# The opening of a two-layer diffusion backbone: the modulation's loads in one run, small products between its matrix products, and another order behind them

## The chip, the cores and the metric

The kernel runs on one core of a Trainium2 chip. The metric is the device time of one execution in microseconds (us); the time given is the median of several runs. TensorE is called PE in the profile, VectorE DVE, ScalarE ACT, GpSimd POOL, and SyncE's queue, which issues all the loads and stores here, SPq.

## The reference

Two layers over 1024 latent tokens and 256 context tokens of width 1024, in float32. What concerns the change is the beginning of a layer:

```python
silu_c = jax.nn.silu(c)
mod = silu_c @ w_ada[l] + b_ada[l]                       # 6 x 1024 values
sh1, sc1, g1, sh2, sc2, g2 = jnp.split(mod[:, None, :], N_MOD, axis=-1)
h = rmsnorm(x, norm1_g[l]) * (1.0 + sc1) + sh1           # the same for the context with c_ctx
y, yc = token_mixers(h @ w_in[l], hc @ w_in[l], ...)     # gated linear memory and neighbourhood attention
x = x + g1 * (y @ w_out[l])
...                                                      # norm2, a squared-ReLU MLP, final norm
```

So no product with `w_in` can start before the sums of squares of x, and the first 2048 columns of `w_ada` (sh1 and sc1), have been worked off.

## The kernel before

Everything lies with features on the partitions: x is 8 feature tiles of 128, and its 1280 tokens are three groups: group 0 the 256 context tokens, groups 1 and 2 the 512 latent tokens each. A float32 product is taken as three (`mm3`, lines 94 to 96): each operand is split into a high part (a cast on ACT, line 1112 or 88) and the rest (a subtraction on DVE, line 1113 or 89), and high x high, high x low and low x high are added up in PSUM.

`opening` (layer 0 only) is ordered by hand: inside it each engine runs its instructions, and SyncE its transfers, in the order in which the code writes them. What comes behind it is ordered by a planner, which may put a later instruction into a place where an engine's queue would wait. `issue_after(i)` holds the instructions traced in its block behind `i`. The opening consists of

- `load_x`: the loads of x by group; `raws`: the first projection's weights `w_kvg` (keys, values and gates of the first head pair) in three pieces, 864, 864 and 576 columns;
- `ada`: two generators, `first` for column blocks 0 and 2 of `w_ada` and `second` for 1 and 3, that is shift and scale of feature tiles 0 to 3 (A) and 4 to 7 (B). Each loads eight tiles of 512 KB ("wada", six buffers for both generators together), multiplies each with silu(c) (line 158), and at its end copies the sums ("arow", line 185), transposes them (line 188) and adds the bias, which gives the columns of `mod` and the gain `A`. `steps(g, n)` takes n steps of a generator; steps 1 to 6 only load, steps 7 and 8 multiply and load, 9 to 14 multiply, 15 ends;
- `squares` (lines 1657 to 1659): the squares of a group on ACT, added in pairs on DVE and summed over partitions by products with ones; `rstd` (lines 297 and 298) takes 1/sqrt of it, `scale` (line 1664) multiplies x by it;
- `norm`: modulates feature tiles, even ones on ACT (line 1676), odd ones on DVE (line 1674), and splits each with `parts`; `self.normed` is the cast of the last one;
- `project`: part of the first projection, by token pair i (256 tokens: pair 0 is group 0, pairs 1 and 2 are group 1, 3 and 4 are group 2), feature tiles ks and half u; a feature tile costs one half three products of 288 columns.

Behind it `mixers` runs: it stores silu(c) to DRAM (`sscr`, two transfers of 1024 single values, line 1590), starts the loads of the further modulation (`fill`), projects token pair 4, turns keys and takes gates (`mlstm_kv`), and projects the values of the attention (`na_values`, weights `w_nv` in two pieces).

Of the kernel before, what the change touches and what calls it, by code (L numbers as in the profile page):

```python
# [11 lines left out]
F32 = mybir.dt.float32  # L12
# [14 lines left out]
KT = D // 128  # L27
# [20 lines left out]
class Kern:  # L48
# [1537 lines left out]
    def mixers(self, l, xsrc, hi, lo, need_ctx, W, accs, Wv):  # L1586
        self.wide = 0
        if l == 0:
            for v in range(2):
                self.nc.sync.dma_start(self.sscr[v, :].rearrange("(k p) -> p k", p=128), self.silu[:, :, v])  # L1590
            self.fill = self.ada(l, range(6, 10), "q")
            self.rows = self.ada_rows(l, range(4, 6), range(2))
        self.gt, self.mst, self.nst = None, {}, {}
        with self.open(name=f"mix{l}", side="right") as self.mx:
            with self.open(name=f"mkv{l}") as self.mp:
                self.cosT = self.load(self.mx, "cos", [128, 8, 32])
                self.sinT = self.load(self.mx, "sin", [128, 8, 32])
                self.sel = self.load(self.mx, "sel", [128, 16])
                kv = self.mlstm_kv(l, hi, lo, W, accs)
                with self.open(name=f"gt{l}", side="right") as tp_:  # L1600
                    gates = self.gates(l, tp_)
                    next(gates)

                    with self.tc.issue_after(self.normed.ins) if l == 0 else contextlib.nullcontext():
                        for i in range(NT // 2):
                            next(kv)
                            if i > 2:
                                next(gates)
                        next(kv)
                    values = self.na_values(l, hi, lo, Wv + self.value_weights(l, range(len(Wv), 2)))  # L1610
                    next(gates)
                    next(gates)
                    run_all(values)
                    with self.behind():
                        run_all(gates)
                W = self.joint_weights(l, 0)
                with self.behind():
                    first = self.project_j(W, 0, hi, lo, 512 if need_ctx else 256)
                with self.open(name=f"mout{l}") as self.mb:
                    self.setup_out(l)  # L1620
                    with self.behind():
                        run_all(kv)
                    Wq, keys = self.mlstm_out(l, hi, lo, need_ctx, W, first)
            with self.open(name=f"na{l}") as self.np_:
                yh, yl = self.alloc_act()
                W, xt = [], []
                self.na(l, hi, lo, need_ctx, Wq, keys, self.ahead(l, 0 if need_ctx else 1, xsrc, yh, yl, W, xt))
        return yh, yl, W, xt

    def opening(self, xp, ap0, xsrc, hi, lo):  # L1630


        nc, d = self.nc, self.d
        self.wide, self.ntmp = 0, 8
        x = self.alloc_x(xp, (0, 1, 2))
        self.setup()
        self.load_x(x, xsrc, (0, 1))
        chunks, raws = ((0, 864), (864, 864), (1728, 576)), []
        for o, n in chunks:
            raws.append(self.wp.tile([128, 1024], F32, name="wraw", bufs=WRAW) if o < 1728 else ap0.tile([128, n], F32, name="wraw2"))  # L1640
        for z in range(2):
            nc.sync.dma_start(raws[z][:, :864], d["w_kvg"][0][:, z * 864:z * 864 + 864])
        first, second = (self.ada(0, blocks, "mm", ap0, 6) for blocks in ((0, 2), (1, 3)))

        def steps(g, n):
            for _ in range(n):
                next(g)

        steps(first, 6)

        def squares(gi, q):
            p, n = self.bank("mm"), GROUPS[gi][1]
            q.extend((p, n))
            for f in range(0, KT, 2):
                sq = [self.sp.tile([128, 512], F32, name="tmp", bufs=self.ntmp) for _ in range(2)]
                for z, t in enumerate(sq):
                    nc.scalar.activation(t[:, :n], xf(x, gi, f + z), AF.Square)
                nc.vector.tensor_add(sq[0][:, :n], sq[0][:, :n], sq[1][:, :n])
                nc.tensor.matmul(p[:, :n], self.ones[:], sq[0][:, :n], start=f == 0, stop=f == KT - 2)
                yield  # L1660

        def scale(gi, r, fs=range(KT)):
            for f in fs:
                nc.vector.tensor_mul(xf(x, gi, f), xf(x, gi, f), r[:, :GROUPS[gi][1]])

        def norm(todo):

            sh = self.mod[:, 0:8, :]

            def modulation(gi, f):  # L1670
                xs, v = xf(x, gi, f), 1 if gi == 0 else 0
                a, b = self.A[0][:, f, v:v + 1], sh[:, f, v:v + 1]
                if f % 2:
                    nc.vector.tensor_scalar(xs, xs, a, b, ALU.mult, ALU.add)
                else:
                    nc.scalar.activation(xs, xs, AF.Identity, bias=b, scale=a)

            modulation(*todo[0])
            for n, (gi, f) in enumerate(todo):
                if n + 1 < len(todo):  # L1680
                    modulation(*todo[n + 1])
                self.normed = self.parts(xf(x, gi, f), hi[f][gi][:], lo[f][gi][:])

        q, A, B, accs = [[], [], []], range(4), range(4, 8), {}

        def project(i, ks, u):
            accs[i] = self.project_g(W, i, hi, lo, "q", accs.get(i), ks, (u,))

        run_all(squares(0, q[0]))
        more = squares(1, q[1])  # L1690
        steps(more, 2)
        r0 = self.rstd(*q[0])
        steps(more, 1)
        steps(first, 1)
        steps(more, 1)
        steps(first, 1)
        self.load_x(x, xsrc, (2,))
        nc.sync.dma_start(raws[2][:], d["w_kvg"][0][:, 1728:])
        r1 = self.rstd(*q[1])
        scale(0, r0)  # L1700
        for z in range(2):
            self.less_last(raws[z], chunks[z][1], 288)
        scale(1, r1, A)
        W = [self.split_raw(raws[z], chunks[z][1]) for z in range(2)]
        scale(1, r1, B)
        for z in range(6):
            steps(first, 1)
            steps(second, 1)
        self.less_last(raws[2], chunks[2][1], 288)
        steps(first, 1)  # L1710
        norm([(0, f) for f in A])
        for u in range(2):
            project(0, A, u)
        rest = squares(2, q[2])
        norm([(1, f) for f in A])
        for i in (1, 2):
            for u in range(2):
                steps(rest, 1)
                project(i, A, u)
                steps(second, 1)  # L1720
        r2 = self.rstd(*q[2])
        W.append(self.split_raw(raws[2], chunks[2][1]))
        steps(second, 4)
        scale(2, r2, range(3))
        steps(second, 1)
        norm([(0, f) for f in B])
        for u in range(2):
            project(0, B, u)
        norm([(1, f) for f in B])
        for i in (1, 2):  # L1730
            for u in range(2):
                project(i, B, u)
        scale(2, r2, range(3, KT))
        norm([(2, f) for f in range(KT)])
        accs[3] = [self.bank("mm") for _ in range(2)]
        for k in range(KT):
            for u in range(2):
                project(3, (k,), u)
        return W, accs, self.value_weights(0, range(1))

    def run(self):
        nc, d = self.nc, self.d
        PS = bass.MemoryType.PSUM
        with self.open(name="pad", side="right") as pad, self.open(name="const") as self.cp, self.open(name="w") as self.wp, \
# [12 lines left out]
            xsrc = d["xT"]  # L1757
            hi, lo = self.alloc_act()
            with self.open(name="x0") as xp, self.open(name="sp0") as self.sp, self.open(name="ada0") as ap0, self.tc.manual_schedule():
                W, accs, Wv = self.opening(xp, ap0, xsrc, hi, lo)  # L1760
            self.ntmp = 3
            for l in range(DEPTH):
                need_ctx = l < DEPTH - 1
                groups = (0, 1, 2) if need_ctx else (1, 2)
                yh, yl, W, xt = self.mixers(l, xsrc, hi, lo, need_ctx, W, accs, Wv if l == 0 else [])
                mod, A = self.mod, self.A
                hid, xmid = hids[l], xmids[l]
                ada = chain(*(self.ada_rows(*a) for a in ((l, range(10, 12), range(2)), (l + 1, range(4), range(2)), (l + 1, range(4, 12), range(1))) if need_ctx))
                hi, lo = self.alloc_act()
# [8 lines left out]
                start, finish = self.down(l, hid, we, alloc)  # L1778
# [110 lines left out]
def run_all(g):  # L1889
    for _ in g:  # L1890
        pass
# [19 lines left out]
WRAW = 2  # L1911
# [128 lines left out]
```

## Time and profile before

| | |
|---|---|
| median of 3 runs | 2864.13 us (2863.14 to 2865.72) |
| the profiled execution | 2859.85 us, of which the span of the profile 2857.9 us |
| instructions | 45593 |
| PE busy | 2807.8 us, 98% of the span |
| DVE, ACT, POOL busy | 2201.7 us, 1276.6 us, 111.9 us |
| DMA | 497.39 MB, mean 174 GB/s |
| granted PE clock, mean | 0.995 |

A row of the order of time has the start in us from the span's start, the duration in us (of a merged run of rows, all of it), the engine, the line, the operation, the tiles written and read, the shape, and how many were merged; the idle time ahead of it and what ended that stand in brackets. Neighbouring products overlap, so their distance is shorter than the duration of one. A row of windows has, for each stretch, the busy us and the number of instructions of each engine, then the granted clock of PE (1.00 is full), the DMA engines' mean busy share and GB/s. A row of waits has the waiting engine and line, what it waited for, the us in total, how many waits, and the longest.

### The profile page before, as it was taken

Reading aid. Unit: us, or ns where it says so; the run is one execution under the profiler, and the core shown is the slowest. Engines: PE = TensorE matmul, PEld = TensorE weight load, DVE = VectorE, ACT = ScalarE, POOL = GpSimd, SP = SyncE. Lnnn points to the kernel's source line nnn. Section 1 sums busy time; section 2 is a strip of 40 time slices with the busy share of each in tenths; the row PEclk is TensorE's granted clock in tenths of the full one; section 3 lists DMA queues with packets and bytes.
Section 4 is the critical chain, followed back from the end, with each engine's and each line's share of the span. In section 5 each row is a group of like instructions: output and inputs, shape, how many; then the busy total and the mean of one; then the engine's idle time right before and its main releaser. Section 6 shows DMA issues by size and latency. Waiting matters only on the chain. (4 is left out here: it accounts for less than half of the span.)

```text
span 2857.9 us, 45593 instructions
## 1 busy us (share of the span) xinstructions
PE 2807.8 (98%) x16560; PEld 2375.8 (83%) x16560; DVE 2201.7 (77%) x4909; ACT 1276.6 (45%) x2472; POOL 111.9 (4%) x191
## 2 busy tenths in 40 slices
PE   7999999999999999999999999999999999999998
PEld 4877778888888888888889988878988788888888
DVE  5779988776698777689878778878786887768774
ACT  4333335565453333434545333335564533344453
POOL 0100000011000000000000101000010000000000
PEclk8999999999999999999999999999999999999999
DMA  7333333336447555798977222223355454479672
GB/s 243 125 132 128 133 104 108 91 114 203 138 149 246 198 195 192 247 341 295 328 264 279 71 70 88 72 76 120 113 156 193 130 183 155 145 263 320 200 256 97
DMA packets 279263, 497.39 MB, mean 174 GB/s; under 512 B 23648, under 2 KB 119904, under 8 KB 279040
## 3 DMA queue, kind: packets, MB, share of 16 engines
q1 hardware_dynamic: 279040, 494.50, 51.8%
q8 instruction: 130, 2.13, 0.3%
q14 instruction: 93, 0.76, 0.1%
HBM read 398.82 MB, written 95.59 MB: 173 GB/s over the span
## 5 line engine op out<-in xcount | busy, mean ns | idle before, releaser
L94 PE MATMUL q<-ah,whi 128*128 128x512 f32 (+1 forms) x1472 | 549.4, 373 | 0.5 <-ACT whi L1112 0.5
L96 PE MATMUL q<-ah,wlo 128*128 128x512 f32 (+1 forms) x1472 | 547.0, 372 | 0.7 <-DVE wlo L1113 0.5
L95 PE MATMUL q<-al,whi 128*128 128x512 f32 (+1 forms) x1472 | 547.6, 372 | 0.0
L94 PE MATMUL mm<-ah,whi 128*128 128x512 f32 (+1 forms) x1120 | 387.0, 346 | 0.4 <-DVE nq L859 0.2
L95 PE MATMUL mm<-al,whi 128*128 128x512 f32 (+1 forms) x1120 | 384.8, 344 | 0.0
L96 PE MATMUL mm<-ah,wlo 128*128 128x512 f32 (+1 forms) x1120 | 384.6, 343 | 0.0
L96 PEld LDWEIGHTS q<-ah,wlo 128*128 128x128 f32 x1472 | 277.3, 188 | 49.9 <-DVE wlo L1113 1.3
L94 PEld LDWEIGHTS q<-ah,whi 128*128 128x128 f32 x1472 | 277.5, 188 | 49.7 <-issue 1.7
L95 PEld LDWEIGHTS q<-al,whi 128*128 128x128 f32 x1472 | 277.5, 189 | 48.4 <-issue 1.4
L94 PE MATMUL mm<-whi,ah 128*128 128x512 f32 (+2 forms) x832 | 308.0, 370 | 1.6 <-ACT va L810 1.6
L95 PE MATMUL mm<-wlo,ah 128*128 128x512 f32 (+2 forms) x832 | 297.9, 358 | 0.4 <-DVE wlo L89 0.3
L96 PE MATMUL mm<-whi,al 128*128 128x512 f32 (+2 forms) x832 | 297.9, 358 | 0.0
L94 PEld LDWEIGHTS mm<-ah,whi 128*128 128x128 f32 x1120 | 212.0, 189 | 28.0 <-issue 2.0
L96 PEld LDWEIGHTS mm<-ah,wlo 128*128 128x128 f32 x1120 | 212.0, 189 | 25.1 <-issue 0.2
L95 PEld LDWEIGHTS mm<-al,whi 128*128 128x128 f32 x1120 | 212.0, 189 | 24.6 <-issue 0.2
L1112 ACT CAST ah<-raw 128x512 fp32r<-128x512 f32 (+1 forms) x264 | 143.5, 566 | 126.0 <-PE q L96 51.8
L1113 DVE TENSOR_TENSOR al<-raw,ah 128x512 fp32r<-128x512 f32 (+1 forms) x264 | 157.8, 622 | 29.9 <-ACT ah L1112 29.2
L94 PEld LDWEIGHTS mm<-whi,ah 128*128 128x128 f32 x832 | 157.1, 189 | 27.1 <-ACT va L810 2.4
L96 PEld LDWEIGHTS mm<-whi,al 128*128 128x128 f32 x832 | 156.9, 189 | 23.8
L95 PEld LDWEIGHTS mm<-wlo,ah 128*128 128x128 f32 x832 | 157.3, 189 | 21.3 <-DVE wlo L89 1.8
L94 PE MATMUL q<-th,whi 128*128 128x512 f32 x384 | 150.4, 392 | 2.1 <-DVE s L1277 2.0
L95 PE MATMUL q<-x,whi 128*128 128x512 f32 x384 | 150.6, 392 | 1.1 <-DVE x L1113 1.1
(306 smaller groups left out, 5237.3 us busy)
## 6 DMA issues: line engine op xcount, KB each, us to landing
raw<-w SPq DMA_DIRECT2D x168, 512.0 KB
raw<-hid SPq DMA_DIRECT2D x104, 512.0 KB
wada<-w_adaT SPq DMA_DIRECT2D x96, 512.0 KB
wraw<-w SPq DMA_DIRECT2D x80, 512.0 KB
hid<-hb SPq DMA_DIRECT2D x128, 256.0 KB
hid<-ht SPq DMA_DIRECT2D x96, 256.0 KB
w<-gscr SPq DMA_DIRECT2D x36, 512.0 KB
wada<-w_ada SPq DMA_DIRECT2D x32, 512.0 KB
```

Of the source, the lines that this page charges most:

```text
L94: mm(out, lh, rh, start=start, stop=False, skip_group_check=True)
L95: mm(out, lh, rl, start=False, stop=False, skip_group_check=True)
L96: mm(out, ll, rh, start=False, stop=stop, skip_group_check=True)
L1112: ins = self.nc.scalar.copy(hi, src)
L1113: self.nc.vector.tensor_sub(lo, src, fview(hi))
```

## The change

In the opening, `second`'s tiles are loaded right behind `first`'s: the load of x's group 2 goes from ahead of them to behind them, and the load of the third piece of `w_kvg` to behind `second`'s fourth tile. `warm(n)` is new: n products of the matrix of ones with the silu tile (128 x 256), written to the bank that token pair 0 will use. One stands behind each of six pairs of steps, one ahead of `first`'s end, and two behind the next two steps of `second`; those are nine in the code. `second`'s products now run ahead of and between the first half's projections, which for pair 1 go feature tile by feature tile; group 2's squares, which ran between the first half's projections, come behind the second half of group 0; the second half of pairs 1 and 2 goes feature tile by feature tile too. The weights of the values are loaded in the opening, but split in `mixers`, behind the second step of the kv loop. The two stores of silu stand in a block `issue_after(self.normed.ins)`. All sums have the same terms in the same arithmetic.

```diff
     def mixers(self, l, xsrc, hi, lo, need_ctx, W, accs, Wv):
         if l == 0:
-            for v in range(2):
-                self.nc.sync.dma_start(self.sscr[v, :].rearrange("(k p) -> p k", p=128), self.silu[:, :, v])
+            with self.tc.issue_after(self.normed.ins):
+                for v in range(2):
+                    self.nc.sync.dma_start(self.sscr[v, :].rearrange("(k p) -> p k", p=128), self.silu[:, :, v])
...
                             if i > 2:
                                 next(gates)
+                            if Wv and i == 1:
+                                Wv = [self.split_raw(Wv[0], 1024)]
...
         q, A, B, accs = [[], [], []], range(4), range(4, 8), {}
+        accs[0] = [self.bank() for _ in range(2)]
 
         def project(i, ks, u):
-            accs[i] = self.project_g(W, i, hi, lo, "q", accs.get(i), ks, (u,))
+            accs[i] = self.project_g(W, i, hi, lo, "q" if i < 3 else "mm", accs.get(i), ks, (u,))
+
+        def warm(n):
+            for _ in range(n):
+                nc.tensor.matmul(accs[0][0][:, 0:256], self.ones[:], self.silu[:].rearrange("p k c -> p (k c)"), start=True, stop=True, skip_group_check=True)
...
-        self.load_x(x, xsrc, (2,))
-        nc.sync.dma_start(raws[2][:], d["w_kvg"][0][:, 1728:])
...
         for z in range(6):
             steps(first, 1)
             steps(second, 1)
-        self.less_last(raws[2], chunks[2][1], 288)
+            warm(1)
+            if z == 3:
+                nc.sync.dma_start(raws[2][:], d["w_kvg"][0][:, 1728:])
+        warm(1)
         steps(first, 1)
+        for z in range(2):
+            steps(second, 1)
+            warm(1)
+        self.load_x(x, xsrc, (2,))
         norm([(0, f) for f in A])
         for u in range(2):
             project(0, A, u)
-        rest = squares(2, q[2])
+        steps(second, 2)
         norm([(1, f) for f in A])
-        for i in (1, 2):
+        for f in A:
             for u in range(2):
-                steps(rest, 1)
-                project(i, A, u)
-                steps(second, 1)
-        r2 = self.rstd(*q[2])
+                project(1, (f,), u)
+            steps(second, 1)
+        self.less_last(raws[2], chunks[2][1], 288)
         W.append(self.split_raw(raws[2], chunks[2][1]))
-        steps(second, 4)
-        scale(2, r2, range(3))
+        project(2, A, 0)
         steps(second, 1)
+        project(2, A, 1)
         norm([(0, f) for f in B])
         for u in range(2):
             project(0, B, u)
-        norm([(1, f) for f in B])
-        for i in (1, 2):
-            for u in range(2):
-                project(i, B, u)
+        run_all(squares(2, q[2]))
+        norm([(1, 4), (1, 5)])
+        r2 = self.rstd(*q[2])
+        scale(2, r2, range(3))
+        norm([(1, 6), (1, 7)])
+        for f in B:
+            for i in (1, 2):
+                for u in range(2):
+                    project(i, (f,), u)
         scale(2, r2, range(3, KT))
         norm([(2, f) for f in range(KT)])
-        accs[3] = [self.bank("mm") for _ in range(2)]
-        for k in range(KT):
+        for f in range(KT):
             for u in range(2):
-                project(3, (k,), u)
-        return W, accs, self.value_weights(0, range(1))
+                project(3, (f,), u)
+        raw = self.wp.tile([128, 1024], F32, name="wraw", bufs=WRAW)
+        nc.sync.dma_start(raw[:], d["w_nv"][0, :, :1024])
+        return W, accs, raw
```

More of the change, by code (lines that the diff above doesn't have):

```diff
@@ L1759, in run @@
             with self.open(name="x0") as xp, self.open(name="sp0") as self.sp, self.open(name="ada0") as ap0, self.tc.manual_schedule():
-                W, accs, Wv = self.opening(xp, ap0, xsrc, hi, lo)
+                W, accs, raw = self.opening(xp, ap0, xsrc, hi, lo)
             self.ntmp = 3
@@ L1764, in run @@
                 groups = (0, 1, 2) if need_ctx else (1, 2)
-                yh, yl, W, xt = self.mixers(l, xsrc, hi, lo, need_ctx, W, accs, Wv if l == 0 else [])
+                yh, yl, W, xt = self.mixers(l, xsrc, hi, lo, need_ctx, W, accs, [raw] if l == 0 else [])
                 mod, A = self.mod, self.A
```

## The prediction

> **What bounds the kernel now.** I read the page first, then the stages, then the queue that issues the loads, then the order of time in the first 80 us.
>
> ```profile
> PE 2807.8 (98%) x16560; PEld 2375.8 (83%) x16560; DVE 2201.7 (77%) x4909; ACT 1276.6 (45%) x2472; POOL 111.9 (4%) x191
> ```
>
> TensorE is busy for 98% of the span, so 50 us are idle, and the change touches only the opening. Its stages, in windows (busy us of PE, PEld, DVE, ACT, POOL, then granted clock, DMA share and GB/s):
>
> ```profile
> 20.00:40.00 20.00, 12.16 (x71) 7.45 (x64) 15.70 (x31) 11.47 (x22) 1.14 (x2) 0.66 1.03 360
> ...
> 24.00:26.00 2.00, 1.72 (x16) 0.20 (x8) 2.00 (x4) 0.00 (x0) 0.00 (x0) 0.50 1.06 389
> ...
> 42.00:44.00 2.00, 2.00 (x13) 0.68 (x12) 0.00 (x0) 0.00 (x0) 0.00 (x0) 0.68 0.33 17
> ...
> 48.00:50.00 2.00, 2.00 (x19) 1.42 (x18) 0.00 (x0) 0.00 (x0) 0.00 (x0) 1.00 0.91 215
> ...
> 84.00:86.00 2.00, 2.00 (x18) 2.00 (x17) 0.45 (x1) 1.62 (x3) 0.00 (x0) 1.00 0.00 0
> ```
>
> Up to about 39 us the transfers are the limit (share 1.03, 360 GB/s) and TensorE's clock is at half for much of it. Then, at 42 to 44, only 17 GB/s move, and the rate comes back at 48. The SyncE queue says why (start, us, line, transfer, count), with a row of its waits and the packets of 36 to 40 us:
>
> ```profile
> 19.13 1.01 SPq L1584 DMA_DIRECT2D x<-xT  x2
> ...
> 21.71 7.19 SPq L174 DMA_DIRECT2D wada<-w_ada  x6
> 30.48 6.91 SPq L1590 DMA_DIRECT2D sscr<-silu  x2
> 37.44 9.62 SPq L174 DMA_DIRECT2D wada<-w_ada  x3
> ```
> ```profile
> SPq L174 <- PE mm L158: 11.4, 7, 2.9
> ```
> ```profile
> DMA packets 2434, 1.01 MB, mean 251 GB/s; under 512 B 1947, under 2 KB 1947, under 8 KB 2434
> ```
>
> The x tiles of group 2 go out at 19.13, ahead of the second half of the modulation; six of its eight tiles follow at 21.71, and then the two stores of silu (sscr, 4-byte pieces) come in between and hold the queue until 37.4. The last two tiles are issued only after that and land behind 48 us. So the second half of the modulation ends late, and this chain sets the end of the opening:
>
> ```profile
> 23.70 1.08 PE L158 MATMUL mm<-wada,silu 128*32 128x256 f32 x8 [0.66 <-DMA wada<-w_ada]
> 25.06 1.08 PE L158 MATMUL mm<-wada,silu 128*32 128x256 f32 x8 [0.28 <-DMA wada<-w_ada]
> 26.26 0.42 DVE L185 COPY arow<-mm 128x256 f32<-128x256 f32 x1
> 28.07 0.60 ACT L1676 ACTIVATE x<-x,mod,A 128x256 f32<-128x256 f32 x1 [6.99 <-DVE A L238]
> 30.61 0.98 DVE L1113 TENSOR_TENSOR al<-x,ah 128x256 fp32r<-128x256 f32 x2
> 34.09 0.29 PE L96 MATMUL q<-whi,al 128*128 128x288 f32 x1
> 34.82 1.46 DVE L1113 TENSOR_TENSOR al<-x,ah 128x512 fp32r<-128x512 f32 x2
> 42.34 1.08 PE L158 MATMUL mm<-wada,silu 128*32 128x256 f32 x8
> 52.41 2.37 PE L158 MATMUL mm<-wada,silu 128*32 128x256 f32 x40
> 55.92 0.41 PE L188 MATMUL mm<-consts,arow 128*128 128x128 f32 x2 [1.14 <-DVE arow L185]
> 56.91 0.60 ACT L1676 ACTIVATE x<-x,mod,A 128x256 f32<-128x256 f32 x1 [4.07 <-DVE A L238]
> 59.45 0.98 DVE L1113 TENSOR_TENSOR al<-x,ah 128x256 fp32r<-128x256 f32 x2
> 60.49 0.19 POOL L516 MEMSET va<- 128x4 f32 x3 [3.36 <-DVE al L1113]
> 74.03 1.47 DVE L1113 TENSOR_TENSOR al<-x,ah 128x512 fp32r<-128x512 f32 x2
> 75.76 1.51 DVE L89 TENSOR_TENSOR wlo<-wraw,whi 128x1024 fp32r<-128x1024 f32 x1
> 77.19 0.48 DVE L513 COPY kt<-q 128x128 f32<-128x128 f32 x2
> 79.81 0.38 PE L94 MATMUL q<-whi,ah 128*128 128x288 f32 x1
> ```
>
> The first half is ready at 28.07, the second at 56.91. From there VectorE works nearly without a gap to 75.50 (the last split of the activations, which I call T), then splits the value weights, and copies kt; the next dense projection starts at 79.81. What brings that last time forward is worth its full length, since TensorE is dense behind it.
>
> **The change, part by part.** Prices, from rows of the same execution:
>
> ```profile
> 44.71 0.29 PE L94 MATMUL q<-whi,ah 128*128 128x288 f32 x1
> 44.84 0.30 PE L95 MATMUL q<-wlo,ah 128*128 128x288 f32 x1
> ...
> 46.00 0.64 PE L158 MATMUL mm<-wada,silu 128*32 128x256 f32 x8
> ...
> 49.77 1.12 PE L1659 MATMUL mm<-tmp,ones 128*128 128x512 f32 x2
> ```
> ```profile
> 35.47 4.26 ACT L1657 ACTIVATE tmp<-x 128x512 f32<-128x512 f32 x8
> 50.93 0.69 ACT L297 ACTIVATE ssq<-mm,eps 128x512 f32<-128x512 f32 x1 [11.20 <-PE mm L1659]
> 51.65 0.63 ACT L298 ACTIVATE ssq<-ssq 128x512 f32<-128x512 f32 x1
> 59.88 0.81 ACT L1676 ACTIVATE x<-x,mod,A 128x512 f32<-128x512 f32 x1
> 60.72 0.62 ACT L1112 CAST ah<-x 128x512 fp32r<-128x512 f32 x1
> ...
> 61.38 0.69 DVE L1113 TENSOR_TENSOR al<-x,ah 128x512 fp32r<-128x512 f32 x1 [0.42 <-ACT ah L1112]
> ...
> 65.05 3.09 DVE L1664 TENSOR_TENSOR x<-x,ssq 128x512 f32<-128x512 f32 x5
> ```
>
> *Loads.* A 512 KB tile lands every 1.36 us (23.70 to 25.06). The second half's tiles now follow tile 7 of the first (25.06) at once, with the 288 KB rest of the gate weights (0.8) after the fourth: tile 3 at 30.5, tile 7 at 36.7. Their buffers come free in time, since tile n of the second half needs product n+2 of the first. The 2 MB of group 2 follow, 42.1; then the value weights, 43.5. The number of transfers is unchanged.
>
> *The first half* stays at 28.07: its copy at 26.26 waits for VectorE's scaling, not for TensorE.
>
> *The added products.* The code has nine of them (6+1+2). None like them is in the trace. The nearest row, ones times 128x512, takes 1.12 for two overlapping passes (49.77); half the columns and one such pass give 0.28. Below: 0, since at full clock 0.57 (a modulation product, below) + 0.28 fits the 1.36 in which TensorE waits for a tile. Above: at half clock 1.08 + 0.55 exceeds 1.36, 0.28 in each of six slots, and three more ahead of the first projections cost 0.3 each: 2.6. I take 0, nearest to the row at full clock, and keep 2.6. They could gain the clock too: the first projections (24 products) ended at 34.4, most of them at half clock; at 0.13 each (44.71 to 44.84) the second token tile's 12 follow the last operand (31.59) in 1.7, 33.4, a gain of 1.0. The row: at 24 to 26 us the clock is 0.50 although TensorE is busy 1.72 of 2 and its gaps are 0.28 to 0.72 long. [...]
>
> *TensorE from 33.4 on*, by program order: products 2 and 3 of the second half (0.47 each in a run of five at 52.41, 0.64 alone at 46.00; I take 0.57), 34.5; the second group's first four feature tiles, 6 products (0.8) each, with products 4 to 7 between them, 40.0 (its operands end at 36.3, tile 7 is there at 36.7); the third token pair, 1.6, 41.6; the transposes. From those to the start of ScalarE's modulation took 0.99 (55.92 to 56.91): the second half is ready at 42.6, not 56.91.
>
> *From there to T*, counted from that moment. Group 0: ScalarE is free at 2.97 (56.91 to 59.88). The squares of group 2, moved here out of the cover of TensorE's work, take ScalarE 4.26, 7.23; the last sum and product follow, 8.0, and the logarithm starts 1.16 behind that product (49.77 to 50.93), 9.2. Meanwhile two tiles of group 1 are modulated and cast (0.81, 2x0.62), 9.3, so it is 9.3; with the exponential 10.65. Three scalings (3x0.62), 12.5; the other two tiles (a modulation, taken as no longer than a cast, and two subtractions of 0.69), 14.5; five scalings, 17.6; then group 2 as before, 68.14 to 75.50, 7.4: 25.0. Before it was 18.6 from the same point, with the squares done ahead of it. T = 42.6 + 25.0 = 67.6, 7.9 earlier. TensorE's 48 products on group 1 and 48 on the next pair lie under this chain (16 us of 25).
>
> *The split of the value weights* moves behind the second step of the kv loop: kt is copied at T + 0.1 instead of T + 1.7, 1.6 earlier. It has to be done before TensorE has run the last token pair, 48 products or 6.4 us; VectorE has over 2 us free there (0.45 of 2 busy at 84 to 86 us), so nothing for it.
>
> *The silu stores* are put under an order behind the last cast. That binds instructions of the cast's engine, ScalarE; the stores are SyncE's. The row of POOL's memset at 60.49 shows it: it stands under the same kind of order and ran 14 us before the last cast. So this edit costs and gives nothing, and the planner places the stores. It put nothing into the queue's waits of up to 2.9 us, and the stores into the one of over 13 (28.9 to the end of product 0 at 42.34). Now the waits for products 0 and 1 of the second half, issued by 28.9, are about 2 us. I take it that the stores follow the loads.
>
> Sum: 7.9 + 1.6 = 9.5 earlier. I take off 1.2 for half-clock windows in the looser stretch from 43 to 68 us (one such window, 3.4 us, costs at most 1.7): 8.3. The profiled execution is 2859.85 for a span of 2857.9, 4.3 below the median 2864.13; the same 8.3 off each gives 2851.5 for it and 2855.8 for the median.
>
> **The rivals.** *The stores stay ahead of the last two tiles.* For it: the edit doesn't hold them, and there is still a wait. Before, 17.5 us pass from their issue at 30.48 until full rate is back at 48, 8.3 of them to drain what was queued. So some 9 to 10 us without payload: tile 7 lands at 46.5, the second half is ready 3.2 later (0.57 + 1.6 + 0.99), T at 74.7, the next projection at 77.4 instead of 79.8. With the fill's tile hoisted along it is 1.4 less: gain 1 to 2.4, about 2862. [...]
>
> *Slower.* The jam lasts as long as there are loads behind it, not a fixed time: then 512 KB in 7 us, the rate of 41 to 48 us, holds for the last two tiles and for group 2. Tile 7 lands at 51 and the 2 MB 28 us later, 79; half the squares and the rest of the chain (20 us) put T near 99, 2886. It decides where tile 7 lands behind 48.9 or the 2 MB behind 57. Against it: the rate came back by itself at 48.
>
> *The gain is given back.* A shift of 9 us changes the planner's order in the 2780 us behind, or a wait for a bank or a load stays where it was: 2860 to 2866.
>
> **How the numbers follow.** Forecast 0.57, with its own range 2853.5 to 2859 (9.5 and 1 at the good end, 3.6 lost to the clock at the bad); stores ahead 0.25; given back 0.10; slower 0.08. The range reaches over the second: 2853.5 to 2863.5. What a measurement can tell is 0.2%, 5.7 us, so faster means below 2858.4: 0.57 x 0.9 + a little of the others = 0.53. Slower: 0.07 + 0.03 = 0.10. Within: 0.37.
>
> **What would show it.** Right: the sscr row behind the two loads of x; the second arow copy near 41 and the second half's first modulation near 42.6; T near 68 and the projection behind it at 70.3; clock 1.00 from 22 to 33. Wrong: sscr between rows of w_ada, under 100 GB/s before 43; a last product of L158 behind 45; a clock of 0.5 at 24 in spite of the added products; VectorE idle between 50 and 60 (the logarithm late); or, with T early, new idle time behind 80.

## The result

Before and after, each timed in 14 runs on one chip: 2863.26 us (2858.01 to 2865.72) and 2857.51 us (2854.02 to 2861.08). The ratio is 0.9983, 95% interval 0.9976 to 0.9991: a gain of 0.17%, 2.6 to 6.9 us, where the forecast had 8.3 and a time of 2855.8. The profiled execution of after took 2859.27 us for a span of 2857.3.

The windows of after that answer to those of before (same columns):

```profile
20.00:40.00 20.00, 19.58 (x162) 11.15 (x161) 14.16 (x28) 8.28 (x15) 1.99 (x3) 1.00 1.05 387
24.00:26.00 2.00, 1.82 (x20) 0.61 (x18) 2.00 (x4) 0.00 (x0) 0.00 (x0) 1.00 1.05 387
...
44.00:46.00 2.00, 1.92 (x11) 1.20 (x9) 0.97 (x3) 1.69 (x5) 0.00 (x0) 1.00 0.55 0
48.00:50.00 2.00, 2.00 (x12) 1.52 (x11) 1.30 (x3) 2.00 (x5) 0.00 (x0) 1.00 0.43 44
```

TensorE's clock is now full from 20 to 40 us (0.66 before), and the transfers run at 387 GB/s throughout (360 before). The stretch with hardly any payload is still there, but at 44 to 52, where nothing waits for a load. SyncE's queue in after:

```profile
25.06 4.77 SPq L174 DMA_DIRECT2D wada<-w_ada  x4
29.88 1.33 SPq L1584 DMA_DIRECT2D x<-xT  x2
...
34.44 6.21 SPq L1591 DMA_DIRECT2D sscr<-silu  x2
```

The stores follow the last tiles and x. The chain that sets the end of the opening, in order of time:

```profile
26.27 1.13 PE L1695 MATMUL q<-silu,ones 128*128 128x256 f32 x4
28.21 0.60 ACT L1679 ACTIVATE x<-x,mod,A 128x256 f32<-128x256 f32 x1 [6.73 <-DVE A L238]
33.70 1.07 PE L158 MATMUL mm<-wada,silu 128*32 128x256 f32 x16
40.36 0.64 PE L158 MATMUL mm<-wada,silu 128*32 128x256 f32 x8
43.58 0.60 ACT L1679 ACTIVATE x<-x,mod,A 128x256 f32<-128x256 f32 x1 [7.30 <-DVE A L238]
46.55 4.27 ACT L1660 ACTIVATE tmp<-x 128x512 f32<-128x512 f32 x8
66.77 1.46 DVE L1113 TENSOR_TENSOR al<-x,ah 128x512 fp32r<-128x512 f32 x2
69.33 1.51 DVE L89 TENSOR_TENSOR wlo<-wraw,whi 128x1024 fp32r<-128x1024 f32 x1
71.39 0.41 PE L525 MATMUL q<-consts,kt 128*128 128x128 f32 x2 [1.94 <-DVE kt L472]
71.99 0.38 PE L94 MATMUL q<-whi,ah 128*128 128x288 f32 x1
```

The second half is ready at 43.58 (before 56.91), 13.3 earlier. The squares, now in the chain, lengthen the way from there to T (the end of the last split, 66.77 + 1.46 = 68.23) from 18.6 to 24.65, so T is 7.3 earlier; the next projection starts at 71.99 instead of 79.81, 7.8 earlier. That is the gain at the end of the opening. Part of it is gone later. Behind 85 us TensorE runs the same products in the same order in both kernels, so each can be set beside its own in the other profile; rows of VectorE and SyncE near 230 and 275 us show it, of before and then of after:

```profile
232.09 0.37 SPq L683 DMA_DIRECT2D w<-gscr  x1
237.38 2.19 DVE L701 SCALAR_TENSOR_TENSOR w<-w,tab,mask 128x128 f32<-128x128 f32 x8 [1.39 <-DMA w<-gscr]
275.41 1.46 SPq L74 DMA_DIRECT2D wraw<-w_j  x2
```
```profile
225.42 0.37 SPq L683 DMA_DIRECT2D w<-gscr  x1
232.03 2.19 DVE L701 SCALAR_TENSOR_TENSOR w<-w,tab,mask 128x128 f32<-128x128 f32 x8 [2.71 <-DMA w<-gscr]
271.41 1.46 SPq L74 DMA_DIRECT2D wraw<-w_j  x2
```

The issue of the decays' load (w<-gscr) is 6.7 earlier in after, the issue of the weights 50 us later only 4.0. Between them VectorE waits 2.71 instead of 1.39 for that load. Of TensorE's lead of 7.8, about 1.1 goes with one half-clock stretch of 3.41 us at 163 us, and 2.7 near 281, where it waits for splits of weights that VectorE now makes late. Of the 4.0 left, 1.0 goes near 2279 us and the rest in small steps, among them half-clock stretches at 665 and 2095 us (about 1.5 each): the two profiled executions end only 0.6 apart, the medians 5.75.

### The profile page after: what moved, and what is told of

It is laid out like the page before. It is cut to its first block, busy times and chain, and to the rows that moved or that the text cites. A ratio compares the mean times of both kernels' runs of the same rounds, so it can differ in the third digit from the quotient of the medians.

```text
span 2857.3 us, 45628 instructions
## 1 busy us (share of the span) xinstructions
PE 2811.5 (98%) x16578; PEld 2375.3 (83%) x16578; DVE 2201.8 (77%) x4909; ACT 1275.9 (45%) x2472; POOL 109.7 (4%) x191
## 3 DMA queue, kind: packets, MB, share of 16 engines
q8 instruction: 131, 2.15, 0.3%
```

## The experiments

All times are in us. "Second half" is the start of its first modulation, "next" the start of the projection behind the opening, "wait" VectorE's wait for w<-gscr near 232 us.

| kernel | second half | T | next | wait | median; before on that chip | ratio to before, 95% interval |
|---|---|---|---|---|---|---|
| before | 56.91 | 75.50 | 79.81 | 1.39 | | |
| after | 43.58 | 68.23 | 71.99 | 2.71 | 2857.51; 2863.26 | 0.9983, 0.9976 to 0.9991 |
| e1: after, no added products | 43.62 | 68.27 | 71.75 | 1.62 | 2854.03; 2861.06 | 0.9977, 0.9968 to 0.9986 |
| e2: before, stores last | 54.52 | 73.11 | 77.52 | 1.57 | 2861.75; 2861.06 | 1.0002, 0.9993 to 1.0011 |
| e3: after, stores ahead | 52.67 | 77.33 | 80.80 | 2.53 | 2866.46; 2861.06 | 1.0023, 1.0014 to 1.0032 |
| e4: after, split later | 43.86 | 68.52 | 71.13 | 2.76 | 2856.21; 2861.06 | 0.9981, 0.9972 to 0.9989 |
| e5: after, loads in old places | 49.54 | 74.19 | 77.67 | 2.71 | 2864.42; 2861.56 | 1.0009, 1.0000 to 1.0018 |
| e6: after, stores without the order | 43.49 | 68.14 | 72.03 | 2.73 | 2857.41; 2861.56 | 0.9990, 0.9980 to 0.9999 |
| e7: before, stores last, squares moved | 47.92 | 75.01 | 79.10 | 1.20 | 2862.68; 2861.56 | 1.0002, 0.9993 to 1.0011 |
| e8: after, no products, squares early, split later | 45.44 | 67.24 | 69.77 | 1.51 | 2855.64; 2861.56 | 0.9978, 0.9969 to 0.9987 |
| e9: before with the added products | 58.70 | 77.27 | 81.29 | 2.58 | 2870.94; 2864.00 | 1.0027, 1.0017 to 1.0036 |
| e10: after, the products in one run at 52 us | 43.62 | 68.27 | 71.95 | 2.18 | 2859.55; 2864.00 | 0.9988, 0.9979 to 0.9996 |
| e11: after, no products, split later | 43.69 | 68.34 | 70.87 | 1.27 | 2855.95; 2864.00 | 0.9974, 0.9963 to 0.9984 |

### Was it the stores that made the second half late?

**e2, the kernel before with its stores at the end of the opening.**

```diff
-            for v in range(2):
-                self.nc.sync.dma_start(self.sscr[v, :]...)      # in mixers
...
+        for v in range(2):
+            nc.sync.dma_start(self.sscr[v, :]...)               # at the end of opening
```

> The kernel before, with the two silu stores written at the end of the hand-ordered opening instead of behind it, so that no load of the opening stands behind them. As the prediction had it, the jam behind the stores makes the second half late: then the second half's first modulation moves from 56.91 us forward by 2 us or more, and the time falls by as much (about 2860). Rival: in the kernel before TensorE's own order (squares and first-half projections ahead of the second half's products, at half clock from 36.5 to 43.3 us) sets it, and tile 7 was never waited for: then the modulation stays within 0.5 us of 56.91 and the time within 1 us of 2863.

The stores go out behind the second half's tiles, no jam comes ahead of them, and the ratio is 1.0002 (0.9993 to 1.0011). Rows of TensorE and ScalarE in e2:

```profile
50.00 2.37 PE L158 MATMUL mm<-wada,silu 128*32 128x256 f32 x40
54.52 0.60 ACT L1674 ACTIVATE x<-x,mod,A 128x256 f32<-128x256 f32 x1 [4.07 <-DVE A L238]
```

Products 3 to 7 run in one stretch of 2.37 without a wait for a tile, as they did in before at 52.41. They come late because TensorE comes to them late: the first half's projections, the wait for the squares (3.47 here) and their products stand ahead of them in its order. The 2.4 us of difference to before I put down to the clock: the second half-clock stretch of before (36.5 to 43.3, clock 0.50) did not occur in this execution. So the jam was real, but in before it did not set the end: by the interval of the ratio, taking it away is worth at most 2.0 us.

**e7, as e2, and group 2's squares behind the second half of group 0.** In the edit `squares(2)`, its `rstd` and the first three scalings move to the place that they have in after; loads and the other products stay.

> The kernel before with the stores of silu at the end of the opening and group 2's squares, their 1/sqrt and the first three scalings moved from among the first half's projections to behind the second half of group 0; loads and the order of the other products stay. Theory (TensorE's own order in front of the second half's products makes the second half late, not the loads): without the wait for the squares (3.47 us) and their products (2.2 us) the second half is ready at 49 to 52 instead of 54.52 with the stores last alone; but the squares now lie in the chain from there to T, which grows from 18.6 to 23 to 25, so T is 73 to 76, as before (75.50), and the median within 2 us of before. Rival (the tiles set it): second half ready at 54 or later, T at 78 or later, median 3 us or more over before.

```profile
43.98 2.37 PE L158 MATMUL mm<-wada,silu 128*32 128x256 f32 x40
47.92 0.60 ACT L1674 ACTIVATE x<-x,mod,A 128x256 f32<-128x256 f32 x1 [11.55 <-DVE A L238]
73.55 1.46 DVE L1113 TENSOR_TENSOR al<-x,ah 128x512 fp32r<-128x512 f32 x2
```

Without the squares ahead of them, the same products run 6.0 earlier and the second half is ready at 47.92, a little before the 49 to 52 of the theory. With e2 this shows that TensorE's own order made it late. And the gain is given away at once: from 47.92 to T it is 27.1 instead of 18.6 (after, with the same squares and its clock at 1.00 on that way, has 24.65; in e7 products of 288 columns start 0.24 apart from 50.2 to 52.4 us and again near 65, instead of 0.13), and the time is that of before.

**e5, after with its loads in the old places** (group 2 of x and the third piece of the gate weights ahead of the second half's tiles):

```diff
+        self.load_x(x, xsrc, (2,))
+        nc.sync.dma_start(raws[2][:], d["w_kvg"][0][:, 1728:])
         r1 = self.rstd(*q[1])
...
-            if z == 3:
-                nc.sync.dma_start(raws[2][:], d["w_kvg"][0][:, 1728:])
...
-        self.load_x(x, xsrc, (2,))
         norm([(0, f) for f in A])
```

> The changed kernel with its loads in the old places: group 2 of x (2 MB) and the third piece of the gate weights go out ahead of the second half's tiles. 2.3 MB at the rate of the changed kernel's loads (512 KB in 1.36 us) are about 6.2 us. Theory (the second half's products wait for their tiles only where these land behind TensorE's other work): the last two tiles land near 42 to 43 instead of 36.7, the second half is ready at 45 to 46 instead of 43.58, the last split of the activations (T) is 1.5 to 2.5 us later than 68.23, median 1.5 to 2.5 us over the changed kernel's. First rival (the place of the loads costs nothing, TensorE's own order sets it): T within 0.7 us. Second rival (the longer waits for tiles draw the stores ahead of the last ones, as where they were put there by hand): sscr between rows of w_ada, T 75 to 77, median 2864 to 2867.

```profile
32.66 1.08 PE L158 MATMUL mm<-wada,silu 128*32 128x256 f32 x8 [5.70 <-DMA wada<-w_ada]
49.54 0.60 ACT L1679 ACTIVATE x<-x,mod,A 128x256 f32<-128x256 f32 x1 [13.95 <-DVE A L238]
```

A miss of mine: I counted on a wait for the last tiles alone. But the second half's first two products stand ahead of the first half's projections in the changed order, so the wait of 5.70 for its first tile moves everything behind it: that product runs 5.1 later than in after (32.66 against 27.56), a half-clock stretch from 28.9 to 35.8 adds 0.9, and the second half and T are 6.0 later. The new order of TensorE needs the new order of the loads.

**e3, after with the stores put by hand behind the sixth tile, ahead of the last two.**

```diff
         steps(first, 1)
+        for v in range(2):
+            nc.sync.dma_start(self.sscr[v, :]...)
         for z in range(2):
             steps(second, 1)
             warm(1)
```

> The changed kernel with the two silu stores put by hand ahead of the second half's last two tiles, where the kernel before has them. By the prediction's rival: tile 7 lands about 10 us later than in the changed kernel, at 46 to 47 us, the second half is ready at 49 to 51 instead of 43.58, T is 5 to 7 us behind 68.23, and most of the gain is gone. If the low rate lasts as long as loads are behind it (the slower rival): group 2 of x lands behind 57 us and the time is above that of the kernel before. If a jam in this place costs little: T within 2 us of 68.23.

```profile
39.98 0.64 PE L158 MATMUL mm<-wada,silu 128*32 128x256 f32 x8 [2.94 <-DMA wada<-w_ada]
45.08 1.08 PE L158 MATMUL mm<-wada,silu 128*32 128x256 f32 x8 [3.26 <-DMA wada<-w_ada]
52.67 0.60 ACT L1676 ACTIVATE x<-x,mod,A 128x256 f32<-128x256 f32 x1 [16.66 <-DVE A L238]
```

Here the jam does set the end: with TensorE's order changed, tiles caught in it cost 9.1 at T, more than the whole gain, and the kernel is slower than before. Of the 9.1, 6.3 is the late tile (45.08, where after has that product at 38.80). The other 2.8 is clock: TensorE waited, its clock was at half from 41.2 to 51.5, and the way from that product to the second half took 7.59 instead of 4.78. This is the first rival of the prediction, made to happen; its price had been put at 7.1 (74.7 against 67.6), with no term for the clock.

### The added products

**e1, after without them** (`warm` runs over `range(0)`).

> The changed kernel without the nine products of ones with silu. If they hold TensorE's clock (theory): the clock falls to half at about 22 us as it did before (22.8), the first half's projections of pair 0 end up to 1.0 us later than the 33.6 of the changed kernel, the second half is ready 1.0 to 1.7 us later than 43.58, and the end of the opening's splits (T) moves from 68.23 by the same. If they do nothing (rival): the clock stays at full without them, T stays within 0.3 us, and only their own 9 x 0.3 us of TensorE are gone. If they cost: T comes earlier.

Two windows of e1, one of after, then rows of ScalarE and VectorE in e1:

```profile
20.43:23.84 3.41, 1.34 (x20) 0.32 (x16) 3.41 (x5) 0.17 (x1) 0.00 (x0) 1.00 1.05 387
24.00:26.00 2.00, 1.73 (x16) 0.32 (x16) 1.86 (x4) 0.00 (x0) 0.00 (x0) 0.50 1.05 386
```
```profile
20.43:23.84 3.41, 3.24 (x29) 1.20 (x24) 3.41 (x6) 1.06 (x2) 0.00 (x0) 1.00 1.05 387
```
```profile
43.62 0.60 ACT L1679 ACTIVATE x<-x,mod,A 128x256 f32<-128x256 f32 x1 [7.32 <-DVE A L238]
66.81 1.46 DVE L1113 TENSOR_TENSOR al<-x,ah 128x512 fp32r<-128x512 f32 x2
```

The products do hold the clock: without them it falls to 0.50 at 23.84 us, with them it is 1.00 from 20 to 40. In the 3.41 us ahead of that TensorE is busy 1.34 without them and 3.24 with them. The 1.73 of 2 behind 24 us is an effect of the half clock, at which a modulation product takes 1.08 instead of 0.64. And holding it buys nothing: the second half and T are where they were, to 0.04, because the first half's projections wait for their operands, and TensorE has caught up at 33.73 (33.70 with them). The longest gap of TensorE between 18 and 24 us in e1 is 0.72. The half-clock stretch behind 23.84 lasts 6.83 us; those of before and after, ahead of 2840 us, last 3.41 (after, from 163.08), 6.83 (before, from 36.46) or 10.24 (before, from 22.81), and each stands behind 3.41 us in which TensorE was busy 1.3 to 2.4; but in after 2.11 of 3.41 from 60.7 us brought none, so the runs give no threshold.

**e9, before with the nine products alone**, put behind the pairs of steps and around the first half's end as in after.

> The kernel before with the nine added products alone: six behind the pairs of steps, one ahead of the first half's end, two behind it. First theory (they hold the clock, and nothing else): clock 1.00 from 22 to 33, the first half's projections about 1 us earlier, the second half ready near 54.5 as with the stores last (where one half-clock window less gave 54.52), T 73 to 74.5 instead of 75.50, the next projection 1 to 2.5 us earlier. Second theory, on what came later: in the five kernels so far with these products the load of the decays (w<-gscr, near 232 us) made VectorE wait 2.5 to 2.8 us, and TensorE lost 2 to 2.7 us near 281; in the five without them the wait was 1.2 to 1.6. If the products' place in TensorE's code does that (a 16 KB piece of code is then fetched about 1.2 us earlier in that load), this kernel waits 2.5 to 2.8 too, and its median is within 2 us of before's. Rival to that (the wait hangs on when the opening ends): 1.2 to 1.6, and the median 1 to 3 us under before's.

```profile
55.74 1.08 PE L158 MATMUL mm<-wada,silu 128*32 128x256 f32 x8 [2.73 <-DMA wada<-w_ada]
58.70 0.60 ACT L1676 ACTIVATE x<-x,mod,A 128x256 f32<-128x256 f32 x1 [7.37 <-DVE A L238]
239.84 2.19 DVE L701 SCALAR_TENSOR_TENSOR w<-w,tab,mask 128x128 f32<-128x128 f32 x8 [2.58 <-DMA w<-gscr]
```

The first theory missed: the clock is full at 24 to 26 us, but T is 1.8 later than before. The planner put a second tile of the further modulation ahead of the second half's last tile (four loads stand in the row behind the stores, three in before), and this last tile came behind the jam; then the clock was at half from 55.3 on (mean 0.52 from 55 to 65 us). The wait near 232 is what the second theory said, 2.58. The end is worse than forecast (ratio 1.0027, 1.0017 to 1.0036); the opening and the stretch near 281 account for 3.4 us of it, the rest, spread over later stages, I did not resolve.

### The order and the split

**e6, after without the block that orders the stores.**

> The changed kernel without the block that puts the two stores of silu under an order behind the last cast. Theory (that block binds ScalarE's instructions, the stores are SyncE's): the sscr rows stand within 0.3 us of 34.44 behind the loads of x and the value weights, T within 0.3 us of 68.23, median within 2 us of the changed kernel's. Rival (the order does hold or place them): without it they go ahead of the last tiles, T 75 to 77, median 2864 to 2867.

```profile
34.45 6.21 SPq L1590 DMA_DIRECT2D sscr<-silu  x2
```

The stores stand where they stood (34.44), T is within 0.1, and the interval of the ratio overlaps that of after: that edit does nothing that can be seen.

**e4, after with the split of the value weights behind the fourth step of the kv loop** (`if Wv and i == 3`).

> The changed kernel with the split of the first value weights behind the fourth step of the kv loop instead of the second. In the changed kernel the 1.51 us subtraction stands between the first rope's products and its sums (69.33 to 70.84) and TensorE waits 1.9 us for that kt. Theory: with the split later this wait goes, the projection of the last token pair starts at about 70.5 us instead of 72, and the 1.5 us stay to the end. Rival: the wait moves to the value projection behind it, which needs the split weights (about 79 us), and nothing is gained.

In after the planner put the split (69.33, 1.51) between the products and the sums of the first rotation of the keys, and TensorE waited 1.94 for kt. In e4 the waits there are 0.6 and 0.3, the next projection starts at 71.13 instead of 71.99. Product set beside product, 0.55 of these 0.86 are left from 82 us on and 0.39 behind 107, and the ratio is that of after.

### Where the rest of the gain goes

The five kernels up to e7 that hold the added products wait 2.5 to 2.8 for w<-gscr, and TensorE loses 2.1 to 2.7 against before near 281; the others wait 1.2 to 1.6 and lose at most 1.1. Rows of the DMA queues (packets, MB, share of 16 engines) for the first four microseconds from the issue of that load: the code queue of after; then of e1 the loads' queue in those four, and both queues in the two microseconds behind them:

```profile
q8 instruction: 1, 0.02, 1.5%
```
```profile
q1 hardware_dynamic: 591, 1.29, 101.1%
...
q1 hardware_dynamic: 201, 0.19, 27.0%
q8 instruction: 1, 0.02, 2.7%
```

In after a packet of the queue q8, which the profile names instruction and I take for code, falls into the load; in e1 there is none in the first four microseconds, and it comes when most of the load has passed (in before too). The whole span of after has 131 such packets with 2.15 MB, so 16 KB each, that of before 130. Counted from its issue, the load is used 1.1 us later in after than in e1 and 1.3 later than in before. The profile of after has 16578 products and as many weight loads, 253 to each packet (before 255); from one packet to the next in after's trace their number varies by 9%, the time by 27% (standard deviations). So I take q8 to carry TensorE's code, an estimate from these counts. With nine products more in that code (18 products and 18 weight loads in the profile) the packet starts 3.3 us behind the issue of the load in after (228.74), where it is 4.6 in before (236.69); in e9 and e10 too it falls into the first four microseconds. VectorE's use of the load follows 6.6 to 6.7 behind the issue in all seven kernels that hold the products, 5.3 to 5.5 in all six without them. The loads' queue in the 1.2 us that begin 5.0 behind the issue, of after and then of e1:

```profile
q1 hardware_dynamic: 27, 0.03, 6.4%
```
```profile
q1 hardware_dynamic: 6, 0.00, 1.1%
```

6.4% of 16 engines is the time of one, and in after's trace the 27 packets follow one another: I take it that one engine's part of the load is still under way behind the packet of code, which took 0.94 us.

The same happens twice more. Rows of VectorE and TensorE, of after and then of e1:

```profile
251.93 1.28 DVE L227 CUSTOM_DVE_ANT_0 wada<-wada,consts 128x1024 f32<-128x1024 f32 x1 [1.34 <-DMA wada<-w_adaT]
2276.84 0.69 DVE L1199 TENSOR_TENSOR sa<-wraw 128x512 f32<-128x512 f32 x1 [2.41 <-DMA wraw<-w]
2279.86 0.50 PE L94 MATMUL q<-ah,whi 128*128 128x512 f32 x1 [1.45 <-ACT whi L1112]
```
```profile
247.71 1.28 DVE L227 CUSTOM_DVE_ANT_0 wada<-wada,consts 128x1024 f32<-128x1024 f32 x1
2271.47 0.69 DVE L1199 TENSOR_TENSOR sa<-wraw 128x512 f32<-128x512 f32 x1 [1.46 <-DMA wraw<-w]
2274.50 0.50 PE L94 MATMUL q<-ah,whi 128*128 128x512 f32 x1 [0.50 <-ACT whi L1112]
```

In after a fetch falls into each of these loads (at 249.89 and at 2272.05). For the first, VectorE waits 0.7 to 1.3 in the seven kernels with the products and not at all in the six without: this is the other half of the 2.7. For the second it waits 1.9 to 2.9 against 1.4 to 1.6, and TensorE loses 0.4 to 3.0 there against at most 0.1.

**e10, after with the nine products in one run behind the squares of group 2**, in the bank of the third token pair, where they can't hold the early clock.

> The changed kernel with the nine added products moved to where they can't hold the clock early: all nine in one run behind the squares of group 2, near 50 us, where TensorE waits for VectorE's chain. The opening's clock then falls at 23 to 24 us as without them, T stays within 0.5 us of 68.27. If the products' number in TensorE's code sets the later wait (second theory): w<-gscr near 231 makes VectorE wait 2.5 to 2.8 us, TensorE loses 2 to 2.7 us near 281, median 2855.5 to 2858. Rival (their place in time, or the clock, sets it): 1.2 to 1.6 us, loss under 1 us, median 2853 to 2855 as without them.

```profile
223.81 0.37 SPq L683 DMA_DIRECT2D w<-gscr  x1
230.46 2.19 DVE L701 SCALAR_TENSOR_TENSOR w<-w,tab,mask 128x128 f32<-128x128 f32 x8 [2.18 <-DMA w<-gscr]
```

The opening is that of e1 (T 68.27, clock at half from 23.9), but the later loss is that of after: the load is late again (used 6.65 behind its issue, after 6.61; the wait is 2.18 and not the 2.5 foreseen since VectorE itself came later), TensorE loses 2.7 near 281, and the ratio is 0.9988 (0.9979 to 0.9996). So it is not the early clock nor the place of the products in time, but that TensorE's code holds them. Over all kernels with the early opening, those with the products (after, e4, e6, e10) have a mean ratio of 0.99855, those without (e1, e8, e11) 0.99763: 2.6 us apart, where a single ratio is known to 0.0007 to 0.0011 on either side; with the errors taken as independent, the 2.6 is an estimate good to about 2.0. That the fetch itself delays the loads is read from the traces; no run moved the fetch and nothing else.

### Better versions

**e8, after without the added products, the split later, and the squares back ahead of the second half of group 0**, summed over features by eight products with ones instead of pairwise sums on VectorE:

```diff
         W.append(self.split_raw(raws[2], chunks[2][1]))
+        ...  # here: 8 squares on ACT, each summed by a product with ones
...
-        run_all(squares(2, q[2]))
```

> A version from the readings so far: the changed kernel without the added products, with the split of the value weights behind the fourth step of the kv loop, and with group 2's squares taken back ahead of the second half of group 0, where ScalarE and TensorE have idle time from 36 to 43 us; they are summed over features by eight products with ones, without the pairwise sums on VectorE. Theory (between 43.6 and T the squares take 4.3 us of ScalarE in the chain): T 64 to 66 instead of 68.23, the next dense projection 10 to 12 us earlier than before instead of 7.8, median 2852 to 2855, ratio to before 0.996 to 0.998. First rival (the last tiles of x land at 42, so the squares end behind 43 and push the second half's modulation back by as much): second half ready at 44.5 or later and T 66.5 to 68. Second rival (VectorE, not ScalarE, carries the chain): ScalarE ends earlier and T stays within 1 us of 68.2.

```profile
43.34 2.19 ACT L1741 ACTIVATE tmp<-x 128x512 f32<-128x512 f32 x4 [0.42 <-DMA x<-xT]
45.44 0.58 ACT L1679 ACTIVATE x<-x,mod,A 128x256 f32<-128x256 f32 x1
65.77 1.47 DVE L1113 TENSOR_TENSOR al<-x,ah 128x512 fp32r<-128x512 f32 x2
```

The first rival came true for the most part: the last four tiles of x land at 43, their squares push the second half's modulation 1.6 behind the gain A (ready 43.8), and T gains 1.0, not the 2.2 to 4.2 of the theory. The late load is not late (1.51), but in the profiled execution TensorE's lead falls from 6.9 to 4.5 with a half-clock stretch of 6.83 us at 663 us, and the ratio, 0.9978 (0.9969 to 0.9987), is that of e1.

**e11, after without the products and with the split later.**

> The changed kernel without the added products and with the split of the value weights behind the fourth step of the kv loop: the best version that the readings give. T 68.2 to 68.3, the next dense projection 8.7 to 9.2 us earlier than before, w<-gscr 1.2 to 1.6 us, median 2852 to 2854.5, ratio to before 0.9965 to 0.998. Rival (the wait for kt is given back at the next weights, as seen with the late split alone): 0.5 to 1 us more near 88 to 90, and the median within 1 us of the kernel without the added products.

The next projection starts 8.9 earlier than before, the wait near 232 is 1.27, and the ratio 0.9974 (0.9963 to 0.9984) is the lowest of all, though its interval overlaps those of e1, e8 and after. The added products can go.

## Why the prediction was right, and where it was not

The forecast of 2855.8 in 2853.5 to 2863.5 holds the 2857.51, which is below the 2858.4 set for faster. Its steps:

- *The first half at 28.07, tile 7 in time, the stores behind the loads, the issue order without effect*: as forecast (28.21; products 3 to 7 without a wait; 34.44; e6). The choice that the stores follow the loads carried all of it: e3 shows 9.1 us on the other side.
- *The cause in before* ("so the second half of the modulation ends late", said of the stores): wrong. e2 took the jam away and gained nothing, e7 moved TensorE's own work and gained 6.6 in the second half. The forecast survived since its sum followed TensorE's order step by step, not the jam.
- *The second half at 42.6*: 43.58. TensorE began at 33.70 (33.4). The mis-sized term is the six projections of a round, taken as 0.8: from 35.68 to 40.36 each round took 1.56, and in it the modulation product 0.57, as taken (35.68 to 36.25), and the six behind it 0.99 (36.25 to 37.24), since the first and the last of them stand 0.24 and 0.21 from the next start instead of 0.13.
- *From there to T 25.0*: 24.65. T is 68.23 instead of 67.6.
- *The split 1.6 earlier*: 0.55 came (7.8 at the next projection, 7.3 at T). The step failed in "nothing for it": it was placed into the chain of kt, and TensorE waited. In e4 the term is there in full (2.61 from T to the next projection, 3.76 in after, 4.31 in before), but more than half of what e4 wins over after is gone by 107 us.
- *The added products at 0*: right for the opening (e1, 0.04 us), and the clock held. Two details were wrong without harm. A product took two passes and 0.56 (x4 and 1.13 for two of them at 26.27), not one of 0.28; with 0.57 this still fits 1.36. And that the clock was at half "although TensorE is busy 1.72 of 2" was read behind its fall: it fell at 22.8, and from 19.4 to 22.8 TensorE was busy 1.73 of 3.4. The 3.6 that the forecast's range loses to the clock at its bad end (the 1.0 of the first projections and the 2.6) is an estimate that no run shows: in e1, with the clock at 0.50 from 23.84 us, T is 68.27, 0.04 behind after. But 2.1 to 2.7 us of loss near 281, and more near 2280, go with the products, which no term of the sum had.
- *1.2 off for half-clock windows from 43 to 68*: that such a stretch lasts 3.4 us fits (3.41 in before from 60.35), but no run shows the 1.2: none came there in after; single ones of 3.41 us came later (163, 665 and 2095 us).
- *Given back*: the planner's order behind 85 us did not change; what was lost was lost to three loads that came late, the decays' first, and to the clock.
- *The slower rival's rate*, "512 KB in 7 us" from 41 to 48: misread. In before 0.26 MB moved in those 7 us (37 GB/s), half of that rate. In after no tile that the opening's modulation needs stood behind the stores.

So 9.5 became 7.8 at the end of the opening. That this is within 0.5 of the forecast 8.3 is in part luck: the 1.2 taken off for the clock was not spent there and made up for most of the 1.7 that the second half and the split fell short. Behind the opening 2.1 to 2.7 went near 281 and 0.4 to 3.0 near 2280, over all kernels with the products, in loads that the prediction had not looked at; the medians keep 5.75 (by the ratio 2.6 to 6.9).

## What to carry to other kernels

A resource that is visibly jammed sets the end only if the instruction that needs it would otherwise run earlier: look first at what stands ahead of that instruction in its own engine's order (e7), and take the jam away alone to see. Edits that belong together can each be worth nothing or less alone: in the kernel before, the stores alone, and the stores with the squares, gained nothing here and the products alone cost 0.27%, and undoing the order of the loads or the place of the stores in the kernel after cost 6 to 9 us in the opening. Instructions added to hold a clock want a run without them: these held it, bought nothing in the opening (T 68.23 with them, 68.27 without), and with them VectorE waited 2.18 to 2.76 us for a load near 232 us instead of 1.20 to 1.62.

## What the runs showed of the hardware

- Two stores of 1024 single values (8 KB in all) held SyncE's queue for 6.21 us and left the DMA at 0 to 49 GB/s in each window of 2 us from 44 to 52 us in after; with tiles of 512 KB caught in the jam (e3), two products that waited for theirs started 5.1 apart (39.98 and 45.08) instead of 1.36.
- TensorE's granted clock fell to 0.50 behind 3.41 us in which the engine was busy 1.34 with no gap over 0.72 (e1); busy 3.24 of the same 3.41 us (after) it stayed at 1.00.
- With 18 products and 18 weight loads more in TensorE's code, placed near 20 or near 52 us, VectorE waited 2.18 to 2.76 us for a load near 232 us in all seven kernels; without them 1.20 to 1.62 in all six. A 16 KB packet on the instruction queue that started 3.3 us behind the issue of that 512 KB load (after), instead of 4.6 (before), went with a use of the load 6.61 behind the issue instead of 5.29.
